# Products on half of the array's rows, in turn on both halves, in a two-block float32 network

## The chip, the cores and the metric

The kernel runs on one core of one Trainium2 chip. The metric is the device time of one execution in microseconds; the time before is 2837.1 us, the median of three runs (2836.09 to 2841.86).

## The reference

Two blocks work on 512 tokens of width 1024, in float32. The first block (a gated recurrent mixer, a Fourier mixer, a convolution and an MLP, two layers) is not touched. The second has two layers, each with three branches, whose outputs are gated and merged. Cut to the lines that the change computes:

```
retention  (4 heads, dk 64, dv 128, chunks of 128)
  scores  = einsum(qc, kc) * decay
  out     = scores @ vc + (qc * decay_q) @ state_before_chunk
gated linear attention  (4 heads, dk 64, dv 128)
  out     = attn(q, k, cumulated gates) @ v + (q * exp(bcum)) @ state
sparse attention  (8 heads in 2 groups, dh 64, 256 keys kept of up to 512)
  logits  = einsum(q, k) / 8, not kept keys at -inf
  out     = softmax(logits) @ v
```

In all three a product contracts over 64 features, which is half of the 128 rows of TensorE's array.

## The kernel before

Weights come from HBM in pieces of 128x1024 and are split into two float32r halves, `whi` by ScalarE (line 283) and `wlo` by VectorE (line 284). A large product is then three float32r products of 512 columns (lines 316 to 318: high by high, low by high, high by low), 24 of them to a tile of 128x512. Other products are in plain float32, and the profile has two MATMUL records and two LDWEIGHTS records for each of these in the program. A form such as `64*128` in the profile means 64 rows and 128 columns of the array.

The second block (`second_block`) runs its branches as generators, called threads here, beside the large products. `gemm_f` and `gemm_t` issue the 24 products and then call `step(2)`, which advances the threads in turn, each to its next `yield`. `finish(thread)` steps without large products until that thread is done. In each layer: the top keys (`select_thread`), the linear attention (`gla_thread`, tg), the sparse attention (`sparse_thread`, td) and the retention (`ret_thread`, tr) are spawned while projections run; then `finish(tg)`, the merge of the linear-attention branch, `finish(tr)`, the merge of retention, `finish(td)`, the merge of the sparse branch. A merge is eight times 24 and 12 products of 512 columns. The framework's scheduler then sets each engine's order by priority; SBUF tiles (`slot`) come from a pool of 57, PSUM banks are 3 named `mm`, 3 named `s` and 2 named `pv`.

A head of the linear attention or the retention ends in `dv_out`: ScalarE squares the PSUM tile (line 1420), VectorE reduces it (1422), scales (1423), GpSimd takes the power (346), VectorE multiplies (1426) and so frees the `pv` bank; two steps later TensorE transposes it (351) and `gate_split` (1411, 312) makes the two halves that the merge reads.

The products that are changed: the sparse scores at line 1735, for each block i of 128 queries and each m of four a pair of heads, e = 0 on rows 0 to 63 and e = 1 on rows 64 to 127, over 128 (i + 1) keys, in plain float32; the retention scores at line 1482 and its state products at 1494; the state products of the linear attention at 1626. The products with the values (1491 and 1623) use all rows. `split(hi, lo, src)` is a ScalarE cast to float32r and a VectorE subtraction (line 312).

Of the kernel before, what the change touches and what calls it, by code (L numbers as in the profile page):

```python
# [2 lines left out]

# [1 line left out]

# [11 lines left out]
P = 128  # L17
# [1306 lines left out]
class Net2(Net):  # L1324
# [132 lines left out]
    def ret_thread(self, tok, v, silu, br):  # L1457
        nc = self.nc
        ft = []
        for i in range(4):  # L1460
            ps = self.tposed(tok[i])
            d = self.slot()
            nc.scalar.copy(d, ps)
            ft.append(d)
            if i % 2:
                yield
        st = {}
        for pr in range(2):
            ps = self.psum("pv")
            for i in range(3):  # L1470
                nc.tensor.matmul(ps[:, :256], tok[i][:, 256 + P * pr:256 + P * pr + P],
                                 v[i][:, 256 * pr:256 * pr + 256], start=i == 0, stop=i == 2, skip_group_check=True)
                d = self.slot((P, 256))
                nc.scalar.copy(d, ps[:, :256])
                st[pr, i + 1] = d
        yield
        for hd in range(4):
            rows = slice(64 * (hd % 2), 64 * (hd % 2) + 64)
            pr = hd // 2
            sp = self.psum("s")  # L1480
            for i in range(4):
                nc.tensor.matmul(sp[:, P * i:P * i + P], ft[i][rows, 256 + P * pr:256 + P * pr + P],
                                 ft[i][rows, P * pr:P * pr + P], start=True, stop=True)
            p = self.slot()
            nc.vector.tensor_mul(p.rearrange("p (i n) -> p i n", n=P), sp.rearrange("p (i n) -> p i n", n=P),
                                 self.mask01.unsqueeze(1).to_broadcast([P, 4, P]))
            yield
            pv = self.psum("pv")

            for i in range(4):  # L1490
                nc.tensor.matmul(pv[:, P * i:P * i + P], p[:, P * i:P * i + P], v[i][:, P * hd:P * hd + P],
                                 start=i == 0, stop=False, skip_group_check=True)
            for i in range(1, 4):
                nc.tensor.matmul(pv[:, P * i:P * i + P], ft[i][rows, P * pr:P * pr + P],
                                 st[pr, i][rows, P * (hd % 2):P * (hd % 2) + P],
                                 start=False, stop=i == 3, skip_group_check=True)
            yield from self.dv_out(pv, hd, br, silu)

    def gla_products(self, l, h):
        nc = self.nc  # L1500
# [11 lines left out]
    def gla_thread(self, l, qk, v, at, silu, br):  # L1512
# [23 lines left out]
        for pr in range(2):  # L1536
# [70 lines left out]
            for i in range(3):  # L1607
# [7 lines left out]
                    nc.vector.scalar_tensor_tensor(d, st[-1], eb[:, i:i + 1], ps[:, :256], op0=OP.mult, op1=OP.add)  # L1615
                st.append(d)
            yield
            for e2 in range(2):
                hd = 2 * pr + e2
                rr = rows[e2]  # L1620
                pv = self.psum("pv")
                for i in range(4):
                    nc.tensor.matmul(pv[:, P * i:P * i + P], sd[e2][:, P * i:P * i + P], v[i][:, P * hd:P * hd + P],
                                     start=i == 0, stop=False, skip_group_check=True)
                for i in range(1, 4):
                    nc.tensor.matmul(pv[:, P * i:P * i + P], x1[rr, P * i:P * i + P], st[i][rr, P * e2:P * e2 + P],
                                     start=False, stop=i == 3, skip_group_check=True)
                yield from self.dv_out(pv, hd, br, silu)
                yield

    def dsa_products(self, l, h):

        nc = self.nc
        kd = self.slot()
        qi = []
        v = self.slot()
        ws = self.wpair(l, 0)
        for i in range(4):
            ps = self.gemm_t(ws, h, i)
            t = self.slot((P, 384))  # L1640
            with self.tc.high_priority():
                nc.scalar.copy(t, ps[:, :384])
                nc.scalar.copy(v[:, P * i:P * i + P], ps[:, 384:])
            self.rope(t, t, i, 6, 8, 32)
            ps = self.tposed(t, 3)
            nc.scalar.copy(kd[:, P * i:P * i + P], ps[:, :P])
            d = self.slot((P, 256))
            nc.scalar.copy(d, ps[:, P:384])
            qi.append(d)
        w = self.wload(self.a["win2_s"][l, 0], 1024)  # L1650
        ps = self.gemm_f(w, 0, P, h, 0, T)
        sm = self.slot()
        nc.scalar.copy(sm, ps)
        return dict(kd=kd, qi=qi, v=v, sm=sm, qd=[], bias=[self.tri[1]])

    def dsa_queries(self, l, h, s):
        nc = self.nc
        ws = self.wpair(l, 1)
        for i in range(4):
# [3 lines left out]
                nc.scalar.activation(t, ps, AF.Copy, scale=0.125)  # L1663
            self.rope(t, t, i, 8, 8, 32)
            ps = self.tposed(t)
            d = self.slot()
            nc.scalar.copy(d, ps)
            s["qd"].append(d)

    def select_thread(self, s):  # L1670
# [50 lines left out]
    def sparse_thread(self, s, silu, br):  # L1721
# [6 lines left out]
        def scores(i, m):  # L1728
# [1 line left out]
            n = P * (i + 1)  # L1730
            c = slice(P * m, P * m + P)
            sps = [self.psum("s") for _ in range(2)]
            for e in range(2):
                rows = slice(64 * e, 64 * e + 64)
                nc.tensor.matmul(sps[e][:, :n], qd[i][rows, c], kd[rows, :n], start=True, stop=True)  # L1735
            mx, sums = self.small("mx", [P, 2], bufs=4), self.small("smx", [P, 2], bufs=4)
            ps = []
            for e in range(2):
# [179 lines left out]
```

## Time and profile before

| | |
|---|---|
| median of three runs | 2837.1 us |
| the profiled execution | 2836.63 us |
| its span | 2834.9 us |
| instructions | 36711 |
| TensorE busy | 2712.0 us, 96% |
| VectorE busy | 1687.2 us, 60% |
| ScalarE busy | 1098.3 us, 39% |
| mean granted clock of TensorE | 0.976 |
| HBM traffic over the span | 110 GB/s |

Busy time of TensorE counts a product from its start to its modelled end, and products are pipelined, so how long a group holds the engine is read from its start to the start of what comes next. The second block begins near 1665 us; layer 0 lies up to 2250, layer 1 behind it.

### The profile page before, as it was taken

To read this page: it belongs to the slowest core of one execution; us is meant where nothing else is said; L and a number is where in the kernel's file an instruction comes from. 1 tells how busy PE (TensorE), PEld (TensorE's weight loads), DVE (VectorE), ACT (ScalarE), POOL (GpSimd) and SP (SyncE) were. 2 spreads that over 40 slices of the span, in tenths; PEclk is the share of its full clock that TensorE was granted. 3 is DMA by queue.
4 is the path that set the end of the run, shared out by engine and by line. 5 is a ranking of instruction groups with operands and counts; after the bars stand their busy time and mean duration, and the time that the engine had idled before them with its cause. 6 is when DMAs were issued, how large, how long until landed. Compare 5 with 4: busy or idle time off the path is not lost.

```text
span 2834.9 us, 36711 instructions
## 1 busy us (share of the span) xinstructions
PE 2712.0 (96%) x13932; PEld 2196.0 (77%) x13932; DVE 1687.2 (60%) x3481; ACT 1098.3 (39%) x2032; POOL 277.7 (10%) x416
## 2 busy tenths in 40 slices
PE   7999998999999998998999999999999999999998
PEld 3888888888888876877888877776788777767887
DVE  3697856577633789965334468666433476674334
ACT  3444536322222464535323353444223443453222
POOL 1152011000000013101000010010011100001011
PEclk9999999999999999998999999999999999999999
DMA  8232323436611653443222242211122422111223
GB/s 301 92 108 85 117 84 125 135 130 207 203 62 60 199 188 98 148 159 118 90 96 96 97 150 70 89 60 38 59 90 95 143 83 83 52 60 45 90 91 118
DMA packets 101281, 312.85 MB, mean 110 GB/s; under 512 B 11504, under 2 KB 15368, under 8 KB 101104
## 3 DMA queue, kind: packets, MB, share of 16 engines
q1 hardware_dynamic: 100544, 309.64, 32.9%
q8 instruction: 109, 1.79, 0.3%
q0 software_dynamic: 560, 0.86, 0.1%
q14 instruction: 68, 0.56, 0.1%
HBM read 293.43 MB, written 17.03 MB: 110 GB/s over the span
## 4 chain that ended last, share of the span: by engine, by line
PE 72%; DVE 14%; DMA 5%; ACT 4%; issue 3%; POOL 2%; SPq 0%; DVEq 0%; POOLq 0%; ACTq 0%
PE mm L317 21%; PE mm L318 20%; PE mm L316 20%; DVE wlo L284 3%; PE s L351 2%; DVE sl L1030 2%; DMA sa<-in_ada 1%; DVE sa L382 1%; PE pv L945 1%; ACT whi L283 1%; DMA sa<-in_w_ada 1%; PE s L1560 1%; POOL rq_y L346 1%; PE s L1735 1%; DMA st<-in_w_mlp 1%
## 5 line engine op out<-in xcount | busy, mean ns | idle before, releaser
L316 PE MATMUL mm<-xhi,whi 128*128 128x512 f32 (+2 forms) x1520 | 596.0, 393 | 15.5 <-DVE sl L1403 7.0
L284 DVE TENSOR_TENSOR wlo<-st,whi 128x1024 fp32r<-128x1024 f32 x352 | 439.1, 1252 | 286.9 <-ACT whi L283 281.1
L283 ACT CAST whi<-st 128x1024 fp32r<-128x1024 f32 x352 | 369.8, 1052 | 617.5 <-PE mm L317 287.1
L317 PE MATMUL mm<-xlo,whi 128*128 128x512 f32 (+2 forms) x1520 | 589.2, 388 | 0.4 <-DVE xlo L312 0.2
L318 PE MATMUL mm<-xhi,wlo 128*128 128x512 f32 (+2 forms) x1520 | 589.0, 388 | 0.0
L316 PEld LDWEIGHTS mm<-xhi,whi 128*128 128x128 f32 (+1 forms) x1520 | 289.8, 191 | 75.2 <-DVE sl L1403 7.8
L318 PEld LDWEIGHTS mm<-xhi,wlo 128*128 128x128 f32 (+1 forms) x1520 | 290.0, 191 | 58.9 <-issue 1.5
L317 PEld LDWEIGHTS mm<-xlo,whi 128*128 128x128 f32 (+1 forms) x1520 | 290.5, 191 | 55.2 <-DVE xlo L312 1.1
L316 PE MATMUL mm<-whi,sl 128*128 128x512 f32 x640 | 250.4, 391 | 2.0 <-DVE sl L697 2.0
L317 PE MATMUL mm<-wlo,sl 128*128 128x512 f32 x640 | 250.4, 391 | 0.7 <-DVE wlo L284 0.6
L318 PE MATMUL mm<-whi,sl 128*128 128x512 f32 x640 | 250.1, 391 | 0.0
L316 PE MATMUL mm<-whi,xhi 128*128 128x512 f32 x576 | 229.6, 400 | 3.9 <-ACT xhi L312 3.9
L317 PE MATMUL mm<-wlo,xhi 128*128 128x512 f32 x576 | 228.1, 396 | 0.2
L318 PE MATMUL mm<-whi,xlo 128*128 128x512 f32 x576 | 227.6, 395 | 0.7 <-DVE xlo L312 0.6
L351 PE MATMUL s<-ident,sl 128*128 128x128 f32 (+2 forms) x748 | 122.8, 286 | 64.9 <-ACT sl L512 17.0
L351 PEld LDWEIGHTS s<-ident,sl 128*128 128x128 f32 (+2 forms) x748 | 87.5, 145 | 115.4 <-issue 39.1
L382 DVE CUSTOM_DVE_ANT_0 sa<-sa,crow 128x1024 f32<-128x1024 f32 x112 | 136.8, 1224 | 35.8 <-DMA sa<-in_w_ada 23.7
L316 PEld LDWEIGHTS mm<-whi,sl 128*128 128x128 f32 x640 | 120.8, 189 | 27.6 <-DVE sl L697 2.4
L317 PEld LDWEIGHTS mm<-wlo,sl 128*128 128x128 f32 x640 | 120.8, 189 | 27.4 <-DVE wlo L284 2.4
L318 PEld LDWEIGHTS mm<-whi,sl 128*128 128x128 f32 x640 | 120.6, 188 | 24.9
L316 PE MATMUL mm<-chi,whi 128*128 128x256 f32 (+1 forms) x448 | 134.0, 300 | 1.1 <-ACT chi L312 1.1
L312 ACT CAST sl<-sl 128x512 fp32r<-128x512 f32 (+2 forms) x144 | 70.6, 500 | 163.6 <-DVE sl L651 120.6
(372 smaller groups left out, 4341.8 us busy)
## 6 DMA issues: line engine op xcount, KB each, us to landing
st<-in_w_mlp SPq DMA_DIRECT2D x128, 512.0 KB
st<-in_win_a SPq DMA_DIRECT2D x116, 512.0 KB
sa<-in_w_ada SPq DMA_DIRECT2D x80, 512.0 KB
sa<-in_ada SPq DMA_DIRECT2D x48, 512.0 KB
st<-in_win_b SPq DMA_DIRECT2D x40, 512.0 KB
st<-in_w_out SPq DMA_DIRECT2D x32, 512.0 KB
xres<-sl SPq DMA_DIRECT2D x48, 256.0 KB
sl<-xres SPq DMA_DIRECT2D x48, 256.0 KB
```

The lines of the kernel that those rows point to most:

```text
L283: nc.scalar.copy(hi, st)
L284: nc.vector.tensor_sub(lo, st, hi.bitcast(F32))
L312: return self.nc.scalar.copy(hi, src), self.nc.vector.tensor_sub(lo, src, hi.bitcast(F32))
L316: mm(ps, l[0], r[0], start=first, stop=False)
L317: mm(ps, l[0], r[1], start=False, stop=False)
L318: self.last_mm = mm(ps, l[1], r[0], start=False, stop=last).ins
L346: self.nc.gpsimd.tensor_tensor(y, v, self.mhalf[:, :n], op=OP.pow)
L351: self.nc.tensor.transpose(out, src, self.ident[:p, :p])
L382: nc.vector.tensor_tensor_reduce(x, st[:, e], row[:, e], 1.0, 0.0, op0=OP.mult, op1=OP.add, accum_out=part[:, m, f, h:h + 1])
L945: nc.tensor.matmul(pvv[:, j], lh, rh, start=m == 0, stop=m == len(mms) - 1)
L1030: nc.vector.scalar_tensor_tensor(accs[f][:, lo:hi], src, w, accs[f][:, lo:hi], op0=OP.mult, op1=OP.add)
L1560: nc.tensor.matmul(sps[e2][64 * u:64 * u + 64, 64 * i:64 * i + 64], kl[rows[e2], e], ql[rows[e2], e], start=True, stop=True)
```

## The change

The sparse scores no longer read plain float32 tiles. The rotated and transposed keys (`kd`) and queries (`qd`) are split into float32r halves, and a pair of heads gets four products each (high and low query by high and low key), in the program's text in turn on rows 0 to 63 and 64 to 127. The retention takes its heads two at a time: scores in turn on both halves, values, state products in turn on both halves, and both `dv_out` side by side, so that a pair of heads makes three steps where two heads made six. The linear attention does the same for its values, state products and `dv_out`, also three steps where there were six.

```diff
--- before.py
+++ after.py
@@ -1,5 +1,6 @@
 import math
 from contextlib import ExitStack
+from itertools import zip_longest
 
 import numpy as np
 
@@ -1474,27 +1475,35 @@
                 nc.scalar.copy(d, ps[:, :256])
                 st[pr, i + 1] = d
         yield
-        for hd in range(4):
-            rows = slice(64 * (hd % 2), 64 * (hd % 2) + 64)
-            pr = hd // 2
-            sp = self.psum("s")
+        rows = [slice(0, 64), slice(64, 128)]
+        for pr in range(2):
+            sps = [self.psum("s") for _ in range(2)]
             for i in range(4):
-                nc.tensor.matmul(sp[:, P * i:P * i + P], ft[i][rows, 256 + P * pr:256 + P * pr + P],
-                                 ft[i][rows, P * pr:P * pr + P], start=True, stop=True)
-            p = self.slot()
-            nc.vector.tensor_mul(p.rearrange("p (i n) -> p i n", n=P), sp.rearrange("p (i n) -> p i n", n=P),
-                                 self.mask01.unsqueeze(1).to_broadcast([P, 4, P]))
+                for e in range(2):
+                    nc.tensor.matmul(sps[e][:, P * i:P * i + P], ft[i][rows[e], 256 + P * pr:256 + P * pr + P],
+                                     ft[i][rows[e], P * pr:P * pr + P], start=True, stop=True)
+            ps = []
+            for e in range(2):
+                p = self.slot()
+                nc.vector.tensor_mul(p.rearrange("p (i n) -> p i n", n=P), sps[e].rearrange("p (i n) -> p i n", n=P),
+                                     self.mask01.unsqueeze(1).to_broadcast([P, 4, P]))
+                ps.append(p)
             yield
-            pv = self.psum("pv")
-
-            for i in range(4):
-                nc.tensor.matmul(pv[:, P * i:P * i + P], p[:, P * i:P * i + P], v[i][:, P * hd:P * hd + P],
-                                 start=i == 0, stop=False, skip_group_check=True)
+            pvs = [self.psum("pv") for _ in range(2)]
+
+            for e in range(2):
+                hd = 2 * pr + e
+                for i in range(4):
+                    nc.tensor.matmul(pvs[e][:, P * i:P * i + P], ps[e][:, P * i:P * i + P],
+                                     v[i][:, P * hd:P * hd + P], start=i == 0, stop=False, skip_group_check=True)
             for i in range(1, 4):
-                nc.tensor.matmul(pv[:, P * i:P * i + P], ft[i][rows, P * pr:P * pr + P],
-                                 st[pr, i][rows, P * (hd % 2):P * (hd % 2) + P],
-                                 start=False, stop=i == 3, skip_group_check=True)
-            yield from self.dv_out(pv, hd, br, silu)
+                for e in range(2):
+                    nc.tensor.matmul(pvs[e][:, P * i:P * i + P], ft[i][rows[e], P * pr:P * pr + P],
+                                     st[pr, i][rows[e], P * e:P * e + P],
+                                     start=False, stop=i == 3, skip_group_check=True)
+            ends = [self.dv_out(pvs[e], 2 * pr + e, br, silu) for e in range(2)]
+            for _ in zip_longest(*ends):
+                yield
 
     def gla_products(self, l, h):
         nc = self.nc
@@ -1615,23 +1624,26 @@
                     nc.vector.scalar_tensor_tensor(d, st[-1], eb[:, i:i + 1], ps[:, :256], op0=OP.mult, op1=OP.add)
                 st.append(d)
             yield
+            pvs = [self.psum("pv") for _ in range(2)]
             for e2 in range(2):
                 hd = 2 * pr + e2
-                rr = rows[e2]
-                pv = self.psum("pv")
                 for i in range(4):
-                    nc.tensor.matmul(pv[:, P * i:P * i + P], sd[e2][:, P * i:P * i + P], v[i][:, P * hd:P * hd + P],
-                                     start=i == 0, stop=False, skip_group_check=True)
-                for i in range(1, 4):
-                    nc.tensor.matmul(pv[:, P * i:P * i + P], x1[rr, P * i:P * i + P], st[i][rr, P * e2:P * e2 + P],
+                    nc.tensor.matmul(pvs[e2][:, P * i:P * i + P], sd[e2][:, P * i:P * i + P],
+                                     v[i][:, P * hd:P * hd + P], start=i == 0, stop=False, skip_group_check=True)
+            for i in range(1, 4):
+                for e2 in range(2):
+                    nc.tensor.matmul(pvs[e2][:, P * i:P * i + P], x1[rows[e2], P * i:P * i + P],
+                                     st[i][rows[e2], P * e2:P * e2 + P],
                                      start=False, stop=i == 3, skip_group_check=True)
-                yield from self.dv_out(pv, hd, br, silu)
+            ends = [self.dv_out(pvs[e2], 2 * pr + e2, br, silu) for e2 in range(2)]
+            for _ in zip_longest(*ends):
                 yield
+            yield
 
     def dsa_products(self, l, h):
 
         nc = self.nc
-        kd = self.slot()
+        kd = (self.slot(dt=F32R), self.slot(dt=F32R))
         qi = []
         v = self.slot()
         ws = self.wpair(l, 0)
@@ -1643,7 +1655,7 @@
                 nc.scalar.copy(v[:, P * i:P * i + P], ps[:, 384:])
             self.rope(t, t, i, 6, 8, 32)
             ps = self.tposed(t, 3)
-            nc.scalar.copy(kd[:, P * i:P * i + P], ps[:, :P])
+            self.split(kd[0][:, P * i:P * i + P], kd[1][:, P * i:P * i + P], ps[:, :P])
             d = self.slot((P, 256))
             nc.scalar.copy(d, ps[:, P:384])
             qi.append(d)
@@ -1663,8 +1675,8 @@
                 nc.scalar.activation(t, ps, AF.Copy, scale=0.125)
             self.rope(t, t, i, 8, 8, 32)
             ps = self.tposed(t)
-            d = self.slot()
-            nc.scalar.copy(d, ps)
+            d = (self.slot(dt=F32R), self.slot(dt=F32R))
+            self.split(*d, ps)
             s["qd"].append(d)
 
     def select_thread(self, s):
@@ -1730,9 +1742,11 @@
             n = P * (i + 1)
             c = slice(P * m, P * m + P)
             sps = [self.psum("s") for _ in range(2)]
-            for e in range(2):
-                rows = slice(64 * e, 64 * e + 64)
-                nc.tensor.matmul(sps[e][:, :n], qd[i][rows, c], kd[rows, :n], start=True, stop=True)
+            for t in range(4):
+                for e in range(2):
+                    rows = slice(64 * e, 64 * e + 64)
+                    nc.tensor.matmul(sps[e][:, :n], qd[i][t // 2][rows, c], kd[t % 2][rows, :n], start=t == 0,
+                                     stop=t == 3)
             mx, sums = self.small("mx", [P, 2], bufs=4), self.small("smx", [P, 2], bufs=4)
             ps = []
             for e in range(2):
```

In the order of TensorE, layer 0, the second retention head stood like this before; `mm` rows are large products, line 351 the transposes of the first head's result, 1482 its scores, 1491 the products with the values, 1494 those with the state.

```order
L316 MATMUL mm_17023<-sl_16940,whi_16973 128x512
L317 MATMUL mm_17023<-sl_16941,whi_16973 128x512
L318 MATMUL mm_17023<-sl_16940,wlo_16974 128x512
L351 MATMUL s_17003<-ident,sl_16952 128x128 x4
L1482 MATMUL s_17014<-sl_16856 128x128
...
L1482 MATMUL s_17014<-sl_16888 128x128
L316 MATMUL mm_17080<-sl_15981,whi_16973 128x512
L1491 MATMUL pv_17062<-sl_15923,sl_17019 128x128
...
L1494 MATMUL pv_17062<-sl_16914,sl_16888 128x128
L317 MATMUL mm_17080<-sl_15982,whi_16973 128x512
```

Of the change, the first pair of retention heads in the same layer (large products are now lines 317 to 319, scores 1483, values 1497, state 1501):

```order
L1483 MATMUL s_17189<-sl_17046 128x128
L1483 MATMUL s_17190<-sl_17046 128x128
...
L1483 MATMUL s_17190<-sl_17108 128x128
L317 MATMUL mm_17237<-sl_16046,whi_17159 128x512
L318 MATMUL mm_17237<-sl_16047,whi_17159 128x512
L319 MATMUL mm_17237<-sl_16046,wlo_17160 128x512
L1497 MATMUL pv_17203<-sl_15982,sl_17199 128x128
...
L1501 MATMUL pv_17203<-sl_17112,sl_17053 128x128
L1501 MATMUL pv_17204<-sl_17112,sl_17053 128x128
```

Both heads now stand in turn, and the group has moved back into the merge: 24 large products stand ahead of its scores, 3 between scores and values, 33 behind its state products, where the second head of before had 1 ahead of its values.

The sparse scores of the last query block in layer 0, first and second pair of heads, on TensorE before:

```order
L1735 MATMUL s_16477<-sl_14108,sl_14688 128x512
L1735 MATMUL s_16478<-sl_14108,sl_14688 128x512
L351 MATMUL s_16499<-ident,sl_16337 128x128
```

and of the change (the first pair, then the start of the second):

```order
L1748 MATMUL s_16640<-sl_14108,sl_14699 128x512
L1748 MATMUL s_16640<-sl_14109,sl_14699 128x512
L1748 MATMUL s_16640<-sl_14108,sl_14700 128x512
L1748 MATMUL s_16640<-sl_14109,sl_14700 128x512
L319 MATMUL mm_17016<-xhi,wlo_17000 128x512
L1748 MATMUL s_16641<-sl_14108,sl_14699 128x512
L1748 MATMUL s_16641<-sl_14109,sl_14699 128x512
...
L1748 MATMUL s_16711<-sl_14108,sl_14699 128x512
L1748 MATMUL s_16712<-sl_14108,sl_14699 128x512
```

The first pair stands head by head, the second in turn. Of the 16 pairs of a layer, the twelve of the first three query blocks and the second of the last block stand in turn; the first, third and fourth of the last block stand head by head.

## Rows read from the trace of the kernel before

**Rows 1.** The page, busy time of each engine: us (share), instructions

```profile
PE 2712.0 (96%) x13932; PEld 2196.0 (77%) x13932; DVE 1687.2 (60%) x3481; ACT 1098.3 (39%) x2032; POOL 277.7 (10%) x416
```

**Rows 2.** The page, chain that ended last, by engine

```profile
PE 72%; DVE 14%; DMA 5%; ACT 4%; issue 3%; POOL 2%; SPq 0%; DVEq 0%; POOLq 0%; ACTq 0%
```

**Rows 3.** Stretches: us, then busy PE, PEld, DVE, ACT, POOL, granted clock, DMA

```profile
1716.00:1790.00 74.00, 72.02 (x315) 56.52 (x313) 71.55 (x186) 27.32 (x38) 0.00 (x0) 1.00 0.26 86
1935.00:2012.00 77.00, 71.27 (x487) 47.39 (x487) 43.12 (x110) 33.53 (x75) 8.00 (x11) 0.91 0.07 22
1996.00:2010.00 14.00, 12.66 (x39) 10.04 (x40) 4.95 (x9) 2.81 (x5) 1.41 (x2) 0.52 0.00 0
2012.00:2060.00 48.00, 48.00 (x234) 39.70 (x233) 18.59 (x25) 11.94 (x16) 2.02 (x2) 1.00 0.24 77
2520.00:2600.00 80.00, 74.15 (x508) 49.61 (x505) 43.67 (x111) 33.54 (x75) 7.72 (x11) 0.94 0.08 28
2583.00:2594.00 11.00, 10.84 (x37) 8.54 (x36) 4.13 (x7) 2.20 (x4) 1.01 (x1) 0.53 0.00 0
```

**Rows 4.** Waits of PE, 1935 to 2012: us in total, times, longest

```profile
PE s L351 <- DVE sl L1426: 3.2, 2, 2.7
PE pv L1471 <- ACT sl L1474: 1.2, 2, 0.7
```

**Rows 5.** Timeline of PE, products on one half: start, us, line, shapes, records

```profile
1977.65 0.93 PE L1626 MATMUL pv<-sl,sl 64*128 64x128 f32 x6
1978.52 1.16 PE L1623 MATMUL pv<-sl,sl 128*128 128x128 f32 x8
...
2015.88 1.16 PE L1482 MATMUL s<-sl 64*128 64x128 f32 x8
2016.96 0.50 PE L316 MATMUL mm<-sl,whi 128*128 128x512 f32 x1
```

**Rows 6.** Chain of waits, 1976 to 2006, end of a linear-attention head: start, us

```profile
1978.68 0.61 ACT sl L1420
...
1981.33 0.70 DVE sl L1426
1982.17 1.50 PE s L351 x12
```

**Rows 7.** Timeline of PE, sparse scores at 128 and 512 keys, and one head alone

```profile
1844.80 0.49 PE L1735 MATMUL s<-sl,sl 64*128 64x128 f32 x4
1845.22 0.97 PE L1560 MATMUL s<-sl 64*64 64x64 f32 x24
...
1936.19 1.13 PE L1735 MATMUL s<-sl,sl 64*128 64x512 f32 x4
1937.26 0.33 PE L351 MATMUL s<-ident,sl 128*128 128x128 f32 x1
...
1948.27 1.12 PE L1735 MATMUL s<-sl,sl 64*128 64x512 f32 x2
1949.33 0.50 PE L316 MATMUL mm<-xhi,whi 128*128 128x512 f32 x1
```

**Rows 8.** Timeline of PE, float32r products over all rows, 256 and 512 wide

```profile
92.57 0.28 PE L318 MATMUL mm<-chi,wlo 128*100 128x256 f32 x1
92.69 0.28 PE L316 MATMUL mm<-chi,whi 128*100 128x256 f32 x1
...
1844.26 0.39 PE L317 MATMUL mm<-wlo,xhi 128*128 128x512 f32 x1
1844.48 0.39 PE L318 MATMUL mm<-whi,xlo 128*128 128x512 f32 x1
```

**Rows 9.** Groups of instructions, VectorE's half of a split: busy us, mean ns

```profile
L312 DVE TENSOR_TENSOR xlo<-sl,xhi 128x512 fp32r<-128x512 f32 x80 | 54.5, 701 | 17.2 <-ACT xhi L312 17.0
...
L312 DVE TENSOR_TENSOR sl<-sl,sl 128x128 fp32r<-128x128 f32 x32 | 8.3, 285 | 0.7 <-ACT sl L312 0.7
```

**Rows 10.** Groups of instructions, 1680 to 1840, transposes waiting for the rotation

```profile
L351 PE MATMUL s<-ident,sl 128*128 128x128 f32 x36 | 6.5, 284 | 3.5 <-DVE sl L1380 3.0 <-POOL sl L254 0.2
```

## The prediction

> **What bounds the kernel now.** I began with the busy times on the page [rows 1]: TensorE is busy 96% of the span, the next engine 60%, so work taken from TensorE counts unless it was beside a wait. The chain that ended last [rows 2] says the same, with TensorE on it 72% of the span and VectorE 14%. The change touches only the second block, so I then cut the trace into its stretches [rows 3]. Three kinds matter. From 1716 to 1790 (choice of the top keys) VectorE is full, 71.55 of 74 us, and TensorE still has work. From 2012 to 2060 TensorE works 48.00 of 48.00 us at a granted clock of 1.00. Between them, from 1935 to 2012, it is idle for 5.7 us and the mean granted clock is 0.91. The low level lies in one piece, 0.52 over 1996 to 2010, that is near 1.2 of 2.4 GHz. Layer 1 repeats this at 2520 to 2600 and 2583 to 2594. The waits of that stretch [rows 4] name the cause: 3.2 us for line 1426 (the end of a head's normalisation, before it is transposed), of which one wait is 2.7 us, and 1.2 us for the retention state. These are threads that run with few large products beside them. What an edit is worth is therefore read in two places: TensorE's own time on the halves, and the waits and the clock of 1935 to 2012.
>
> **Products over half the rows.** A product in plain float32 stands as two records. The state products of one linear-attention head take 1977.65 to 1978.52, 0.87 us, and the retention scores of one head 2015.88 to 2016.96, 1.08 us [rows 5]. Does a second head on the other half cost more? The sparse scores of before answer it [rows 7]: two heads at 512 keys, four records, take 1936.19 to 1937.26, 1.07 us; one head by itself, two records, takes 1948.27 to 1949.33, 1.06 us. So two heads cost what one costs, provided that they stand alternately. The new order has them so in both threads. Removed: 8 pairs (4 linear attention, 4 retention) of state products at 0.87, 7.0 us, and 4 pairs of retention scores at 1.08, 4.3 us. Together **-11.3 us**, all on TensorE's path; 0 if they did not overlap, which the 1.07 against 1.06 makes unlikely.
>
> **Fewer steps of the threads.** A pair of heads now ends in three steps where it took six. In the loop that steps threads without large products between them the linear attention thus ends earlier, and nearly the whole retention thread falls behind it, into the merge. The order of TensorE shows it: the second retention head stood with 1 large product ahead of its value products, the first pair now has 24 ahead of its scores and 33 behind its values. In the merge there is no idle time [rows 3], so the 2.7 us wait for line 1426 and the 1.2 us for the state are covered by products of 0.23 us each: 3.9 us in each layer, -7.8. What is late next is the last linear-attention pair. It holds both pv buffers, and the sparse values behind it need one. A buffer comes free after square, reduction, power and multiplication, 1978.68 to 1982.03, 3.4 us [rows 6], and I add one reduction of the second head, 0.7: 4.1 us. The order has 9 transposes (1.50 us for 12, so 1.1) and 8 large products (1.8) in between, 2.9 in all. The new wait is 1.2, in two layers +2.4. Net **-5.4 us**; -7.8 if cover is complete, 0 if the waits only change names.
>
> **The clock.** In the two low stretches TensorE was busy 12.66 and 10.84 us at 0.52 and 0.53 [rows 3]. At full clock this work would take 6.1 and 5.1 us less. The low level came after the head that waits 2.7 us; in 2012 to 2060, with large products, it is 1.00. I take two thirds of 11.2 back, **-7.5 us**, since the stretch ahead of the merge stays short of large products; bounds 0 and -11.2.
>
> **Sparse scores.** 32 pairs of heads, 8 each at 128, 256, 384 and 512 keys. Before, 128 keys took 1844.80 to 1845.22, 0.42 us, and 512 keys 1.07 [rows 7]; a straight line gives 0.64 and 0.85 between them, and 0.21 that does not grow with the keys (the first weight load and the way out, half each by estimate). Now each half has four float32r products. Over all rows these follow each other at 0.12 us for 256 columns and 0.227 for 512 [rows 8], weight load included; 0.17 at 384 is an estimate between them, and at 128 I take 0.12 as well, because the load may be the floor (the line would give 0.067). No row shows float32r on half the rows. If halves overlap as in plain float32, a pair costs 0.21 plus four products: 0.69, 0.69, 0.90, 1.12, or +0.27, +0.05, +0.05, +0.05 a pair. At 512 keys the scheduler did not keep the alternation: of four pairs in a layer only the second alternates. The first now takes eight in a row, 0.21 + 1.82 = 2.03 against 1.07; the third and fourth were already apart at 2 x 1.06 = 2.12. Sum: 8 x 0.27 + 16 x 0.05 + 2 x 0.05 + 2 x 0.96 - 4 x 0.09 = **+4.6 us**. With 0.067 at 128 keys it is +2.9. With no overlap the pairs cost 1.17, 1.17, 1.59 and 2.03, and the sum is 8 x 0.75 + 8 x 0.53 + 8 x 0.74 + 2 x 0.96 + 1.6 = +19.6.
>
> **Splits.** VectorE gets 8 subtractions of 128x512 at 0.70 us and 8 of 128x128 at 0.285 [rows 9], 7.9 us. Most hide: VectorE is no bound outside 1716 to 1790, and there TensorE does not wait for the top keys. The three later query tiles of a layer are rotated in that full stretch, though, and transposes wait 3.0 us for rotation [rows 10]. Each may start up to 0.70 later: at most 2.1 a layer. I take a third, **+1.4 us**; bounds 0 and +4.2. ScalarE's copies become casts of the same tiles, one for one, and SP's order is the same row for row.
>
> **Sum.** -11.3 - 5.4 - 7.5 + 4.6 + 1.4 = -18.2 us. The profiled execution took 2836.6 us (span 2834.9), 0.5 under the median of 2837.1. 2836.6 - 18.2 + 0.5 gives **2819 us** on the scale of the median. The best of all bounds is -11.3 - 7.8 - 11.2 + 2.9 + 0 = -27.4, or 2809.7.
>
> **Rivals.**
> *Halves in turn.* Float32r on half the rows hides its loads but does not overlap: +19.6 instead of +4.6, 2834 us. For it: no row of before has such a product. Against it: the same halves overlap in plain float32 [rows 7].
> *Neither overlap nor hidden loads.* Line 1748 runs its eight products one after the other, and each shows its own load of 0.10 us (half of the 0.21 above). That adds 8 x 0.10 = 0.8 us to each of 32 pairs, 25.6, on top of 19.6: +45 in place of +4.6, about 2860 us, slower. It decides the sign once the sparse scores cost 28 us more than before, 0.88 us a pair. Against it: over all rows each product has its own load and still follows at 0.12 [rows 8]. The Trainium skill speaks for it: "TensorE: Matmul & The Clock Gate", Part 3, What overlaps and what doesn't, says that a weight load overlaps running products only where the row group differs. By that rule the four products of a half would each show their load, unless the other half's product covers it; the trace of before disagrees for products on all rows, where group and load are the same and nothing shows.
> *The waits come back.* Clock and waits reappear elsewhere (threads of the linear attention and of the sparse values wait for two pv buffers and three s buffers): these two terms are 0, and -11.3 + 4.6 + 1.4 = -5.3 leaves 2832 us. For it: two heads take their buffers at once. The skill warns of this too ("TensorEngine Tiling (Array Packing)", Gotcha 1: row tiles write different PSUM banks, so pressure rises); what it would make here is these 12.9 us given back. Against it: at three of four pairs in a layer the order has 24 or more large products, 5.4 us, behind a pair, more than the 4.1 that a buffer is held.
>
> **How the numbers follow.** Forecast (2809 to 2829) 0.70; waits come back 0.12; halves in turn 0.10; neither overlap nor hidden loads 0.08. A difference of 0.2%, 5.7 us, is about what a measurement can tell: same is 2831.4 to 2842.8. Halves in turn falls there; waits come back lies on its edge and is shared equally. Faster 0.70 + 0.06 = 0.76, same 0.16, slower 0.08. The range is 2809 to 2838: it takes in the two middle cases, with room for new waits, and leaves out the last.
>
> **What would show it.** In the trace after: six-record groups of state products for two heads (twelve records) in about 0.9 us; line 1748 at 0.7 to 1.1 us a pair where it alternates and 2.0 where it does not; no wait over 1 us for the retention heads and a granted clock of 1.00 around them; a wait near 1.2 us ahead of the sparse values behind the last linear-attention pair. I am wrong if line 1748 takes over 1.2 us a pair at 128 keys, if a low level of the clock of 10 us or more stands near 1990 and 2580 again, or if TensorE's idle time from 1935 on in a layer grows past 5.7 us.

## The result, and the profile after

Before took 2838.4 us (median of 4 runs), the changed kernel 2807.6 (2802.0 to 2811.8, 4 runs): ratio 0.9894, interval 0.9877 to 0.9911, 30.8 us less. 2819 was forecast, with 2809 to 2838 as the range, so this median lies 1.4 us under it. Measured again on another chip (below) the ratio was 0.9911 (0.9894 to 0.9928), 24.3 us less. The direction and the places were as forecast; the gain was larger.

The profiled execution is the longest of its four, 2811.75 us. Its page gives the busy times and the chain, beside [rows 1] and [rows 2]:

```profile
PE 2697.8 (96%) x14060; PEld 2194.9 (78%) x14060; DVE 1693.0 (60%) x3497; ACT 1096.9 (39%) x2032; POOL 276.2 (10%) x416
...
PE 69%; DVE 16%; DMA 7%; ACT 4%; issue 3%; POOL 2%; SPq 0%; DVEq 0%; POOLq 0%; ACTq 0%
```

TensorE has 128 records more and is busy 14 us less; the bound is the same. The two layers of the second block as stretches, first of before, then of after (columns as in [rows 3]):

```profile
1663.00:2248.00 585.00, 565.72 (x2967) 437.16 (x2967) 323.71 (x700) 227.16 (x412) 57.71 (x85) 0.98 0.25 82
2248.00:2834.00 586.00, 564.11 (x2954) 435.07 (x2954) 319.08 (x687) 216.84 (x391) 55.97 (x80) 0.98 0.24 80
```

```profile
1667.00:2238.00 571.00, 556.22 (x3031) 437.28 (x3031) 326.63 (x706) 226.22 (x410) 57.16 (x85) 0.98 0.26 84
2238.00:2810.00 572.00, 554.30 (x3018) 434.86 (x3018) 321.95 (x695) 216.21 (x391) 55.64 (x80) 0.98 0.25 82
```

Both layers together take 1171 us before and 1143 after, 28.0 less. TensorE's idle time falls from 41.2 to 32.5, so 8.7 of the 28 are waits. The untouched first block took 3.5 us more in this execution, which is why the spans differ by 24.9 only.

The stretches that answer to [rows 3], now around the linear attention's end and the retention:

```profile
1940.00:1996.00 56.00, 54.57 (x385) 38.02 (x384) 33.10 (x84) 29.55 (x67) 5.72 (x9) 1.00 0.12 39
1996.00:2012.00 16.00, 16.00 (x97) 13.00 (x96) 5.71 (x10) 3.77 (x7) 1.98 (x2) 1.00 0.10 35
...
2566.00:2600.00 34.00, 34.00 (x204) 28.14 (x203) 15.25 (x23) 10.09 (x16) 1.99 (x2) 1.00 0.19 62
```

From 1996 to 2012 TensorE is busy without a break at a granted clock of 1.00, where [rows 3] had 0.52. The waits of the first layer, 1667 to 2238 (who waits, for whom, us, times, longest), beside [rows 4] and [rows 10]:

```profile
PE s L352 <- DVE sl L1381: 3.7, 4, 1.8
...
PE pv L1783 <- DVE sl L1427: 1.0, 1, 1.0
...
PE pv L1631 <- DVE sl L1791: 0.4, 1, 0.4
PE s L352 <- DVE sl L1769: 0.4, 1, 0.4
```

Before, this layer also had a wait for a rotation on GpSimd:

```profile
PE s L351 <- POOL sl L251: 0.8, 1, 0.8
```

The retention's waits (3.2 and 1.2 us) and this one are gone. The forecast new one, sparse values (L1783) behind the last linear-attention pair, stands at 1.0. The waits for rotation are 3.7 against 3.0 in [rows 10]; in the second layer they are 1.9 against 2.9.

The products on TensorE's timeline (start, us, line), beside [rows 5] and [rows 7]:

```profile
1975.33 0.94 PE L1635 MATMUL pv<-sl,sl 64*128 64x128 f32 x12
1976.19 0.98 PE L352 MATMUL s<-ident,sl 128*128 128x128 f32 x7
...
2002.83 1.16 PE L1483 MATMUL s<-sl 64*128 64x128 f32 x16
2003.92 0.50 PE L317 MATMUL mm<-sl,whi 128*128 128x512 f32 x1
...
1851.16 0.66 PE L1748 MATMUL s<-sl,sl 64*128 64x128 f32 x8
1851.75 0.44 PE L1569 MATMUL s<-sl 64*64 64x64 f32 x6
...
1946.19 1.19 PE L1748 MATMUL s<-sl,sl 64*128 64x512 f32 x4
1947.32 0.50 PE L319 MATMUL mm<-xhi,wlo 128*128 128x512 f32 x1
1947.75 1.19 PE L1748 MATMUL s<-sl,sl 64*128 64x512 f32 x4
...
1955.61 1.19 PE L1748 MATMUL s<-sl,sl 64*128 64x512 f32 x8
1956.73 0.44 PE L352 MATMUL s<-ident,sl 128*128 128x128 f32 x2
```

From a group's start to the next: twelve records of two heads' state products 0.86 us (one head's six took 0.87), sixteen of scores 1.09 (eight took 1.08), a pair of sparse scores 0.59 at 128 keys (0.42 before) and 1.12 at 512 (1.07). So float32r products on the two halves overlap too. At the first pair with 512 keys a large product stands between the two heads' four products: each four then take 1.13 us by themselves, as much as all eight at 1955.61.

The third pair with 512 keys takes 2.14 us, 1959.46 to 1961.60. The profile shows why, in the weight loads of its two heads: the second head waits for VectorE's line 1573, which reads its bank.

```profile
1959.46 0.76 PEld L1748 LDWEIGHTS s<-sl,sl 64*128 64x128 f32 x4
1960.46 0.77 PEld L1748 LDWEIGHTS s<-sl,sl 64*128 64x128 f32 x4 [0.24 <-DVE sl L1573]
```

In the last pair of this layer, too, the second head starts at 1967.57, right behind ScalarE's line 1777, which reads its bank up to 1967.53. The first head's fourth product starts only at 1967.64, though the program's order has it ahead of the second head.

The products that build the retention state, of before and then of after, where large products stand between them:

```profile
1990.08 0.70 PE L1471 MATMUL pv<-sl,sl 128*128 128x256 f32 x2
1991.24 0.70 PE L1471 MATMUL pv<-sl,sl 128*128 128x256 f32 x2 [0.46 <-ACT sl L1474]
...
1992.99 0.70 PE L1472 MATMUL pv<-sl,sl 128*128 128x256 f32 x2
1993.34 0.58 PE L319 MATMUL mm<-sl,wlo 128*128 128x512 f32 x1
```

Before, two of them hold TensorE for 1.16 us from start to start, less 0.46 of wait, 0.70; after, a large product starts 0.35 behind them.

Where the 28.0 us of the second block went. For each record of TensorE I took the time from its start to the next one's start, less the idle time ahead of that one, and counted time in low-clock pieces half:

| us in the second block | before | whole change | pairs only | state products apart |
|---|---|---|---|---|
| retention scores | 9.3 | 5.2 | 5.2 | 5.2 |
| retention state products | 6.8 | 3.5 | 3.5 | 6.9 |
| linear attention, values and state products | 15.5 | 12.5 | 13.3 | 15.5 |
| sparse scores | 28.1 | 31.7 | 25.8 | 31.7 |
| building the retention state (L1471, after L1472) | 6.7 | 3.8 | 3.8 | 3.8 |
| all records of TensorE | 1106.0 | 1093.3 | 1089.2 | 1102.7 |

The overlap gives -10.4, the sparse scores +3.5, the retention state -2.8. Idle time gives -8.7 (stretches above). TensorE was busy 47.0 us in low-clock pieces before and 33.7 after; half the difference is -6.6. These make -25.0; the other 3.0 are spread over lines of which none gave more than 1.

### The profile page after: what moved, and what is told of

Its sections match the earlier page's. It is cut to its first block, busy times and chain, and to the rows that moved or that the text cites. A ratio compares the mean times of both kernels' runs of the same rounds, so it can differ in the third digit from the quotient of the medians.

```text
span 2810.0 us, 37002 instructions
## 1 busy us (share of the span) xinstructions
PE 2697.8 (96%) x14060; PEld 2194.9 (78%) x14060; DVE 1693.0 (60%) x3497; ACT 1096.9 (39%) x2032; POOL 276.2 (10%) x416
## 4 chain that ended last, share of the span: by engine, by line
PE 69%; DVE 16%; DMA 7%; ACT 4%; issue 3%; POOL 2%; SPq 0%; DVEq 0%; POOLq 0%; ACTq 0%
PE mm L318 19%; PE mm L319 19%; PE mm L317 19%; DVE wlo L285 3%; PE s L352 2%; DMA sa<-in_w_ada 2%; DVE sa L383 2%; DVE sl L1031 2%; DMA sa<-in_ada 1%; ACT whi L284 1%; PE s L1569 1%; PE s L1748 1%; PE pv L946 1%; POOL rq_y L347 1%; PE pv L1783 1%
## 5 line engine op out<-in xcount | busy, mean ns | idle before, releaser
L317 PEld LDWEIGHTS mm<-whi,xhi 128*128 128x128 f32 x576 | 109.3, 190 | 30.8 <-ACT xhi L313 6.5
```

The costliest lines, as they stand in the source:

```text
L317: mm(ps, l[0], r[0], start=first, stop=False)
```

## The experiments

Medians are set against the kernel before on the same chip. A second measure helps, since the runs of one kernel differ by up to 0.7%: the loss of clock, each run's span times one minus its mean granted clock, and the time less this loss. Means over all runs of a kernel:

| kernel | runs | us | loss of clock | us less loss | second block, profiled runs |
|---|---|---|---|---|---|
| before | 45 | 2837.0 | 69.9 | 2767.1 | 1171.2 |
| whole change | 10 | 2809.3 | 64.0 | 2745.3 | 1142.8, 1141.6 |
| pairs only | 9 | 2801.4 | 58.2 | 2743.2 | 1135.3, 1135.2 |
| sparse scores only | 12 | 2841.2 | 67.0 | 2774.2 | 1171.7 |
| six steps | 12 | 2840.7 | 73.1 | 2767.6 | 1176.8 |
| head by head | 5 | 2806.5 | 56.1 | 2750.4 | 1142.4 |
| retention pairs only | 6 | 2823.5 | 60.2 | 2763.3 | 1160.1 |
| linear-attention pairs only | 6 | 2814.8 | 61.0 | 2753.9 | 1147.5 |
| sparse scores apart | 10 | 2804.1 | 56.9 | 2747.2 | 1141.9, 1139.6 |
| state products apart | 11 | 2810.0 | 56.7 | 2753.3 | 1147.5, 1148.4 |

One run's loss spreads by 3 to 9 us (standard deviation), the time less loss by 2 to 4. The last column is read from the traces: from the transposes that wait 4.6 us for ScalarE (1663.70 before, 1667.21 after), with which the second block begins in every kernel, to the end of the span. Up to these transposes TensorE has the same records in all fourteen traces, and yet they start anywhere from 1659.0 to 1671.0 us: 12 us of the difference between two profiled runs can lie in work that no edit touched. Where a kernel was profiled twice, the second block alone agrees within 0.1 to 2.3 us.

**Pairs only** (twice). Sparse scores as before:

```diff
...
-            for t in range(4):
-                for e in range(2):
-                    rows = slice(64 * e, 64 * e + 64)
-                    nc.tensor.matmul(sps[e][:, :n], qd[i][t // 2][rows, c], kd[t % 2][rows, :n], start=t == 0,
-                                     stop=t == 3)
+            for e in range(2):
+                rows = slice(64 * e, 64 * e + 64)
+                nc.tensor.matmul(sps[e][:, :n], qd[i][rows, c], kd[rows, :n], start=True, stop=True)
```

> The kernel before with the heads of retention and linear attention in pairs (alternating halves, three steps a pair instead of six); the sparse scores stay in plain float32, whole. Theory A, by which the two traces split the gain as overlap -11.3, covered waits -5.8, clock -11.2, sparse scores +3.6: this kernel is 28 us under the kernel before, some 3 to 4 us under the whole change. Rival B, the float32r sparse scores are themselves a gain: it stays 3 us or more over the whole change, at about -25 or less against before.

> The pairs with the sparse scores in plain float32, again. Theory (float32r sparse scores cost 3.5 us): 3 to 4 us under the whole change, the fastest of the four. Rival (float32r sparse scores cost nothing, or save VectorE or ScalarE time): the same as the whole change or above it.

2804.4 (0.9879, 0.9859 to 0.9899), then 2800.0 (0.9871, 0.9855 to 0.9888) beside 2811.7 of the whole change. It is the fastest version, ahead of both kernels; in the second comparison the intervals of the two do not overlap. Its TensorE records take 4.1 us less than the whole change's and 3.6 less in the second pair of profiles, as the theory has it. Of the 11.7 us of the second comparison about 9.8 are loss of clock (means 65.1 and 55.3), so the size of the step between the two is less sure than its sign; the second block alone is 7.5 and 6.4 us shorter than the whole change's. Its sparse scores take 25.8 us, less than before's 28.1, because the last pair of a layer takes 1.06 us in this order and took 2.37 before.

**Sparse scores only.** The kernel before with the lines that are marked - in the fence above, and with the splits of keys and queries.

> The kernel before with only the sparse scores changed (float32r halves, four products a head, the heads in pairs). Theory A: +4 us against before (27 more us of VectorE's and TensorE's records in all, of which the pairs show 3.6); line 1748's place is taken by pairs of 0.6 to 1.1 us that start 3 to 4 ns apart. Rival B, gain through VectorE or ScalarE work that moved: -3 us or less. Rival C, halves in turn: +15 to +20.

2841.8, ratio 1.0017 (1.0005 to 1.0028), +5.4 us by the medians (7.1 in the time less loss). In the profiled run TensorE's records take 6.6 us more, 4.9 of them the sparse scores; its second block is only 0.5 us longer, because 5.0 less is lost to the clock there. The float32r sparse scores cost time; the price without overlap (15 to 20) is excluded.

**Six steps.** Whole change with three empty steps behind each pair, in both threads:

```diff
+            for _ in range(3):
+                yield
```

> The whole change with three empty steps more behind each pair of heads in retention and linear attention, so that the two threads take as many steps as before while their products alternate. Theory A (about 17 us of the gain come from where the retention thread stands, 11 from the overlap): -8 against before, with the waits of retention and the low granted clock near 1996 and 2583 back. Rival B, the overlap alone gives the gain and the order of steps nothing: -25 or more, no different from the whole change.

2840.0, 1.0014 (1.0000 to 1.0028), so -8 was wrong and the rival (-25) more so. The waits of TensorE from 1960 to 2015, and the stretches there, show why:

```profile
PE s L352 <- DVE sl L1427: 8.5, 2, 4.5
PE pv L1472 <- ACT sl L1475: 1.0, 2, 0.5
```

```profile
1980.00:1995.00 15.00, 10.51 (x64) 8.79 (x62) 7.17 (x13) 5.78 (x12) 2.00 (x2) 0.77 0.11 36
1995.00:2010.00 15.00, 9.99 (x66) 7.63 (x66) 5.98 (x11) 3.47 (x8) 1.98 (x2) 0.86 0.00 0
2010.00:2025.00 15.00, 14.09 (x72) 11.48 (x69) 4.56 (x7) 2.93 (x5) 0.00 (x0) 0.80 0.11 36
```

8.5 us of waiting for two heads normalised at once, against 3.2 in [rows 4], and the clock is low again. In the second block the records take 6.7 us less than before, idle time 10.4 more: the overlap is there and the waits eat it. Pairs in the old place are worth nothing. This run does not price the steps alone, since two heads that end together wait longer than two that end in turn.

**Head by head.** Whole change, loops over the halves and the tiles exchanged in scores and state products:

```diff
...
-            for i in range(1, 4):
-                for e in range(2):
+            for e in range(2):
+                for i in range(1, 4):
...
```

> The whole change, but the retention scores and the state products of retention and linear attention issued head by head (first half's products, then the second's); steps and buffers in pairs as in the whole change. Theory A: the 11.3 us of overlap are lost and the 17 us of steps stay, so -13 to -18 against before; two heads' state products take about 1.75 us again, scores 2.15. Rival B, the steps are worth nothing: +4 against before. Rival C, TensorE overlaps the halves though they stand apart: no different from the whole change.

2807.2, 0.9891 (0.9875 to 0.9907): nearest to rival C. The timeline:

```profile
1968.33 1.26 PE L1635 MATMUL pv<-sl,sl 64*128 64x128 f32 x12
1969.52 0.65 PE L352 MATMUL s<-ident,sl 128*128 128x128 f32 x4
```

1.19 us for twelve records, not 1.75: the first record of the second head starts 0.33 us in, beside the third of the first head's six, and the two run side by side from there. The theory of steps and waits was thus not separated from the overlap here.

**State products apart** (twice). The second head's values, over all rows, stand between the two heads' state products:

```diff
             for e in range(2):
                 hd = 2 * pr + e
                 for i in range(4):
                     nc.tensor.matmul(pvs[e][:, P * i:P * i + P], ps[e][:, P * i:P * i + P],
...
-            for i in range(1, 4):
-                for e in range(2):
+                for i in range(1, 4):
...
```

> The whole change, but within a pair the value products (all rows) of the second head stand between the state products of the two heads, so that the halves of the state products are never neighbours; steps and buffers as in the whole change. Theory A, the overlap is on the path that sets the end: +6 us against the whole change (state products of the second block 13 us again instead of 6.9), about -24 against before. Rival B, the overlap is not on that path and all the gain is where the retention thread stands: no difference from the whole change, -30 against before.

> The whole change with the state products of the two heads kept apart by the value products, again. Theory, the overlap lies on the path that sets the end: +6 us against the whole change (its trace shows 6.4 us more in those products). Rival, it does not: the same as the whole change.

2810.5 (0.9896, 0.9879 to 0.9914), then 2810.9 (0.9912, 0.9898 to 0.9926): by the time alone the same as the whole change, as the rival has it. Yet its records take 9.4 us more and its time less loss 8.0; the loss of clock is 7.3 us lower. The second block of its two profiled runs is 4.7 and 6.8 us longer than the whole change's beside it, near the +6 of the theory, and 23 to 24 under before's. So the overlap lies on the path, though the medians do not show it; why the loss is lower stays open (seven us between two means each good to about two).

**One thread at a time.** Retention pairs alone, linear-attention pairs alone, each against the kernel before, with the diff of its thread.

> The kernel before with only the retention heads in pairs (alternating halves, three steps a pair). Theory A, now: overlap of retention -7.4 (scores 9.3 to 5.2 us, state products 6.8 to 3.5), the waits and the low granted clock are tied to where the retention thread stands, and that is set by how soon the linear-attention thread ends, which is as before here: most of waits and clock stay, -8 to -14 against before. Rival B, the fewer steps of retention itself cover its waits: -20 or more.

> The kernel before with only the linear-attention heads in pairs. Theory A: overlap -3 us, and the linear attention ends earlier, so that retention moves under the merge's large products: its waits (9 us of idle time in the second block) and the low granted clock (7 to 11 us) go with it: -18 to -25 against before. Rival B, retention's own steps cover its waits: -3 to -6 only.

Retention alone: 2824.2, 0.9947 (0.9933 to 0.9961), -14.7. Linear attention alone: 2817.2, 0.9912 (0.9893 to 0.9932), -21.8. The waits from 1960 to 2015 and the stretches, of retention alone:

```profile
PE s L352 <- DVE sl L1427: 4.1, 3, 3.2
PE pv L1497 <- DVE sl L1488: 1.7, 2, 1.4
```

```profile
1999.00:2005.00 6.00, 4.08 (x27) 3.27 (x28) 4.35 (x8) 1.73 (x3) 0.32 (x1) 0.72 0.00 0
2576.00:2587.00 11.00, 7.51 (x40) 6.66 (x40) 5.85 (x9) 1.73 (x3) 1.84 (x2) 0.55 0.01 1
```

and of linear attention alone:

```profile
PE pv L1773 <- DVE sl L1427: 1.0, 1, 1.0
PE s L352 <- DVE sl L1759: 0.4, 1, 0.4
```

```profile
2000.00:2020.00 20.00, 20.00 (x101) 16.34 (x101) 8.99 (x12) 5.36 (x7) 1.01 (x1) 1.00 0.20 65
2560.00:2600.00 40.00, 40.00 (x198) 32.52 (x197) 15.63 (x23) 14.67 (x26) 1.01 (x1) 1.00 0.25 79
```

This tells the theory from its rival, for the waits. Pairs of retention gain 9.0 us in records and leave the waits; idle time even grows by 4.1. The low clock stays beside the retention too (0.72 and 0.55), but for a shorter time in layer 0, and the second block gains 6.1 us from the clock, more than the theory allowed (TensorE is busy 34.6 us in low-clock pieces there, 47.0 before); the mean loss of its six runs is 9.7 under before's, and its time less loss only 3.8 under. Pairs of linear attention, which do not touch retention's code, take away its waits, bring 1.00 and shorten the building of its state from 6.7 to 3.8 us. In the second block their records take 7.9 us less (2.8 the building of the state, 2.3 the sparse scores, whose last pair stands as in pairs only, 2.2 the linear attention itself), idle time is 5.9 less, and the clock gives 9.8 (27.3 us busy in low-clock pieces). It is the earlier end of the linear attention that moves retention under the large products.

**Sparse scores apart** (twice). Whole change, four products of one half and then four of the other:

```diff
-            for t in range(4):
-                for e in range(2):
-                    rows = slice(64 * e, 64 * e + 64)
+            for e in range(2):
+                rows = slice(64 * e, 64 * e + 64)
+                for t in range(4):
```

> The whole change with the sparse scores issued head by head, four float32r products of one half and then four of the other. If TensorE starts a later half only when three or four records are left of the first, as it does for the state products issued head by head: pairs of about 0.76, 0.9, 1.2 and 1.6 us at 128 to 512 keys instead of 0.59, 0.67, 0.89 and 1.12, and +6 to +8 us against the whole change, -23 against before. Rival, no overlap at all in this order: +15 against the whole change, -15 against before. Rival, TensorE sorts it out wholly: no difference from the whole change.

> The whole change with the sparse scores head by head, again. By its trace TensorE runs the two halves side by side in this order as well (0.60 to 1.14 us a pair) and saves 0.8 us, at the fourth pair with 512 keys: the same as the whole change within 2 us. Rival, its first result (2802 us) was more than chance: 5 us or more under the whole change.

2802.0 (0.9882, 0.9862 to 0.9901), then 2802.3 (0.9885, 0.9867 to 0.9903). The timeline at 128 and 512 keys:

```profile
1855.05 0.67 PE L1748 MATMUL s<-sl,sl 64*128 64x128 f32 x8
1855.65 0.33 PE L1569 MATMUL s<-sl 64*64 64x64 f32 x2
...
1972.15 1.21 PE L1748 MATMUL s<-sl,sl 64*128 64x512 f32 x8
1973.29 0.66 PE L352 MATMUL s<-ident,sl 128*128 128x128 f32 x4
```

0.60 and 1.14 us a pair: TensorE runs four and four side by side in this order as well, and my estimate of a part overlap was wrong. At 128 keys the second half's first product starts 14 ns behind the first half's, where alternating halves start 3 ns apart; the scheduled order of this run is not listed. Its second median lies 9.4 us under the whole change's beside it, as the rival has it, though the intervals overlap. The time less loss does not differ in its favour (2747.2 against 2745.3), and the second block is only 0.9 and 2.0 us shorter, so most of the difference is loss of clock (56.9 against 64.0) and not work that this order saves; whether the loss is chance stays open.

**The whole change again**, beside these:

> The whole change again, beside the next three on one chip, since they differ by less than two separate comparisons can tell. Expected: -29 to -32 us against before. By the profiled runs so far the time without the clock's loss (span times one minus the mean granted clock) falls by 22 and the loss itself by 6 to 12.

2811.7 (2804.5 to 2817.0, 6 runs), 0.9911: 24.3 us less, under the -29 expected. Over all ten runs of the whole change, against the means of before, the time less loss falls by 21.8 and the loss by 5.9. The second block of the two profiled runs is 28.4 and 29.6 us shorter.

## Why the prediction was right and where it was wrong

- **The bound and the places**: right. TensorE stays the bound, and the gain is in its own records and in the stretch of the retention.
- **Overlap of half-row products, -11.3**: right, -10.4 by the records. With the state products apart they take 6.4 us more again. The condition, that the halves stand alternately, is too strict: head by head, part of the overlap stays.
- **Fewer steps, -5.4**: the step that failed, in its size, and with it the lower end of the range, for which this term stood at -7.8 at best. The sentence "3.9 us in each layer, -7.8" counted two waits. Gone are the whole 3.2 and 1.2 of [rows 4] and 0.8 for a rotation on GpSimd, in both layers 10.4; new are 1.0 as forecast (1.2) and 0.9 at two other places, 3.7 in both layers. With gaps too short for the list, idle time fell by 8.7. The retention state also became cheaper by 2.8: its products had stood alone between copies of ScalarE, a cost that shows in the distance of their starts and only partly as a wait, and I did not look there. Together -11.5, where the sum had -4.0 (this term and the splits). Linear-attention pairs only shows both effects without a change to retention's code.
- **Splits, +1.4**: about nothing. Rotation waits went from 3.0 to 3.7 in one layer and from 2.9 to 1.9 in the other.
- **Clock, -7.5**: right in place; the size is near by luck. The pair of profiles gives -6.6, the means of all runs -5.9, but in the other kernels with three steps a pair, in one thread or both, the mean loss is 8.9 to 13.8 under before's. Both low stretches are gone, not two thirds of them, but others (near 1815 and 2385) come and go with the run. Low clock beside the retention, 3.4 to 17.0 us a layer, stands in the four traces in which the linear attention ends late (before, sparse only, six steps, retention pairs only) and in none of the other ten. That the waits cause it is argued, not shown: no run changed the clock alone, and retention pairs only keeps the waits and yet has a mean loss 9.7 under before's.
- **Sparse scores, +4.6**: right, +3.5. At 128 keys the pair takes 0.59, not 0.69: the products follow at 0.11 us, little under the 0.12 that was taken, and the part that does not grow is 0.15 (0.59 less four times 0.11), not 0.21. Where the order broke up the alternation, the first pair took 2.24 (2.03 forecast), the third 2.14 and the last 1.6 to 1.9 (2.03 each). The last had taken 2.37 before, not 2.12. The lost alternation is not what these two pay for: the second head's bank is read late (1960.46 and 1967.57, above), and with the sparse scores apart the last pair, in the text head by head as well, takes 1.14. In the rival's sum 1.59 at 384 keys should be 1.57, which takes 0.2 off its 19.6.
- **Rivals**: halves in turn, and neither overlap nor hidden loads, are excluded by the 0.59 and 1.12 of line 1748 and by sparse scores only (+5.4). The Trainium skill ("TensorE: Matmul & The Clock Gate", Part 3, What overlaps and what doesn't) says that a weight load overlaps running products only where the row group differs. This trace does not agree: four products of one half with nothing of the other beside them take 1.13 us (1946.19), as long as eight alternating ones, and start 0.23 us apart behind the first, like the full-row products of [rows 8], so their loads do not show. The waits did not come back; that rival needs the six-step order.

So the forecast of -18.2 had the signs right and missed 7.5 us of waits and of the building of the retention state, and 3.0 us spread over lines that it had not listed. Measured again, the ratio of 0.9911 makes 2811.9 us on the forecast's scale, inside the range; that the first median lies 1.4 us under it is within the noise, but the size of this term was wrong in both profiles of the whole change.

## What to carry to other kernels

When threads share an engine, ask first which thread ends earlier and what then stands beside the next one: pairs in one thread paid mostly by moving another thread under large products, and the same pairs with the old number of steps gained nothing. Read a wait's cost from the distance of starts of the products around it, not only from the list of waits. And where runs spread by 0.5%, compare the time less the loss of clock as well, and the stretch that the edit touches by itself, or a change of 6 us on the path can vanish in the medians.

## What the runs showed of the hardware

- TensorE does not need products on the two halves to alternate. Four float32r products of one half followed by four of the other took 0.60 us at 128 columns and 1.14 at 512, against 0.59 and 1.12 alternating. Nor do products of the two halves start in the program's order: in the last pair of layer 0 the second half's first product starts at 1967.57, the first half's fourth, which stands ahead of it, at 1967.64. The second half must be free to start, though: where its bank was still being read, the pair took 2.14 at 512 columns. In plain float32, where a product is two records, it reaches less far: six and six records took 1.19 instead of 0.86, eight and eight 1.64 instead of 1.09. With eight full-row records in between there is no overlap (6.9 us for eight heads' state products against 3.5).
- The loss of clock differed between runs of one kernel by more than the whole sparse term: in the ten runs of the whole change the mean granted clock was 0.974 to 0.982, that is 50 to 73 us of loss.
